# Attention keys in 512-token tiles with both parts one under the other, queries as two tiles with each part twice

## The chip, the cores and the metric

The kernel runs on one core of one Trainium2 chip. The metric is the device time of the program in microseconds (us), as the median of three runs. Its engines are TensorE (PE in the profile; its weight loads are PEld), VectorE (DVE), ScalarE (ACT), GpSimd (POOL) and SyncE (SP), which issues the DMA transfers.

## What is computed

One layer of a streaming encoder, for a prompt of 1024 tokens and for a sample of 64 tokens with cached keys and values. The part that matters here is the first attention. A combined projection gives queries, keys and values for 16 heads of 64 dimensions. Eight heads (A) attend in a band: each 64-frame chunk sees itself and the eight chunks before it. Eight heads (B) are causal over the whole prompt, with a bias from cumulated forget gates. Cut to these lines:

```python
p = rms_norm(x, g_norm1) @ w_in            # q_A k_A v_A | q_B k_B v_B | forget logits
qa, ka = rms_norm(heads(...), g_qa), rms_norm(heads(...), g_ka)     # the same for qb, kb

def attend(q, k, v, bias, mask):
    logits = einsum('bqhd,bkhd->bhqk', q, k) * HEAD_DIM ** -0.5 + bias
    logits = where(mask, logits, -inf)
    return einsum('bhqk,bkhd->bqhd', softmax(logits), v)

# A, prompt: chunk c (64 frames) against frames c*64-512 .. c*64+63, learned relative bias
# B, prompt: query t against frames 0..t, bias cum[t] - cum[s], cum = cumsum(log_sigmoid(forget))
# sample:    64 queries against the cache (512 keys in A, 1024 in B) and the 64 new keys
x = x + concat(oa, ob) @ w_o
x = x + memory_cross_attention(x, mem)     # 4 heads, 256 memory tokens
x = x + conv_ffn(x)
```

The prompt and the sample use the same weights. Keys and values of both go to the outputs too.

## The kernel before

**Parts.** All matmuls run in fp32r, with each operand in two parts: `hi` is the value rounded to fp32r and `lo` is what is left of it. A product of two such values is made of the products hi·hi, hi·lo and lo·hi (in the scores lo·lo as well).

**Head pairs and token tiles.** The prompt's attention goes over eight head pairs `p` (0 to 3 are A, 4 to 7 are B) and eight tiles `t` of 128 tokens. For each, `proj` makes the projection of the tile for the two heads: 24 matmuls into the PSUM bank `pj` (L272, inside `one`). Then `qk_norm` normalizes queries and keys into `qk`, which holds each head's 64 dimensions twice, side by side, so that the transposes in `turn` (L293) give 128 partitions with the dimensions one under the other twice. `gained` (L237 on ScalarE, L238 on VectorE) multiplies them by a gain, rounds them into `hi` and subtracts for `lo`; its last argument limits `lo` to some partitions.

**Groups.** A `Group` holds 256 tokens of a head pair. Keys lie in `kh` (hi in both halves of the partitions) and `kl` (lo in both halves). Queries lie in one tile `q`: hi in partitions 0 to 63, and lo, which is written in place over the second copy, in partitions 64 to 127. One matmul of `q` with `kh` so gives q_hi·k_hi + q_lo·k_hi, and one with `kl` the two other products.

**Scores.** `Attn.score` makes the scores of one tile of 128 queries of a head against its window of `n` keys (up to 640 in A, up to 1024 in B). It walks the key groups of 256 tokens and has two matmuls for each, with `kh` and with `kl` (L453), so at most 256 columns each. They go into `S`, a PSUM tile of two banks that there is only once. A reduction on VectorE (L456) adds the bias, puts the result in `s` and finds the maximum `mx`; ScalarE makes the exponentials (L458). Then come transposes of the probabilities (L493) and the sums with the values.

**Order.** `substeps` cuts the attention of an earlier 256-token group into small functions, and `weave` puts them between the projection matmuls of the next token tile. The last score steps of a pair run beside the next pair's projection. The order on each engine is settled by a scheduler that takes the program in the order of this code and moves instructions by their dependencies. The first pair runs to about 120 us, the others to 571 us.

**Memory and samples.** Next, eight `Sample` units, one for each head pair, and the projection of the memory's keys and values (`mem_piece`, L615) run woven with each other, from about 600 to 722 us. `splitk` takes the cached keys of a head from the input in pieces of 512 tokens; they lie there with the dimensions twice over 128 partitions. ScalarE copies a piece into `kchi` (L709) and VectorE subtracts for `kclo` (L710). `Sample.score` multiplies the two heads' queries (`sq_`, hi over lo, in the trace with a number) with `kchi` of each piece and the new keys' `skn0`, and then with `kclo` and `skn1` (L730, L731). An A sample has one piece for each head, a B sample two. Behind 722 us come the output projection, the memory attention and the ConvFFN.

## Time and profile before

| | |
|---|---|
| three runs | 1797.77, 1800.52, 1801.03 us |
| median | 1800.52 us |
| profiled execution, its own time | 1798.58 us |
| its span, first to last instruction | 1796.5 us |
| mean granted clock of TensorE in it | 0.991 of full speed |

The profile is that of one execution of 1798.58 us. Of this the span is 1796.5 us; the other 2.08 us lie around it. All rows below count from the span's start. A row of a matmul gives its busy time from its start to a modelled end. Since matmuls overlap in the pipeline, the distance from one start to the next is shorter than that time.

### The profile page before, as it was taken

Reading aid. Unit: us, or ns where it says so; the run is one execution under the profiler, and the core shown is the slowest. Engines: PE = TensorE matmul, PEld = TensorE weight load, DVE = VectorE, ACT = ScalarE, POOL = GpSimd, SP = SyncE. Lnnn points to the kernel's source line nnn. Section 1 sums busy time; section 2 is a strip of 40 time slices with the busy share of each in tenths; the row PEclk is TensorE's granted clock in tenths of the full one; section 3 lists DMA queues with packets and bytes.
Section 4 is the critical chain, followed back from the end, with each engine's and each line's share of the span. In section 5 each row is a group of like instructions: output and inputs, shape, how many; then the busy total and the mean of one; then the engine's idle time right before and its main releaser. Section 6 shows DMA issues by size and latency. Waiting matters only on the chain.

```text
span 1796.5 us, 34030 instructions
## 1 busy us (share of the span) xinstructions
PE 1718.8 (96%) x12412; PEld 1663.7 (93%) x12412; DVE 1225.0 (68%) x2710; ACT 930.5 (52%) x2042; POOL 662.8 (37%) x1025
## 2 busy tenths in 40 slices
PE   6899999999997888999999999999999999999999
PEld 5789999999997777999999999999999999999999
DVE  5877667677676797433444379877777777677994
ACT  5646666677676567433554456343333333433332
POOL 5746657878776554453443612100000000000000
PEclk9999999999999999999999999999999999999999
DMA  8312122122113777541111563222222222794232
GB/s 285 96 46 72 36 76 79 50 72 74 48 54 97 222 229 213 163 141 60 54 54 59 150 219 103 73 79 78 85 86 84 73 73 72 268 304 151 77 118 80
DMA packets 134103, 200.12 MB, mean 111 GB/s; under 512 B 20824, under 2 KB 73944, under 8 KB 133936
## 3 DMA queue, kind: packets, MB, share of 16 engines
q1 hardware_dynamic: 133936, 197.96, 34.9%
q8 instruction: 97, 1.59, 0.4%
q14 instruction: 70, 0.57, 0.1%
HBM read 155.61 MB, written 45.44 MB: 112 GB/s over the span
## 4 chain that ended last, share of the span: by engine, by line
PE 46%; DVE 3%; DMA 2%; issue 2%; POOL 1%; ACT 1%; SPq 0%; POOLq 0%; ACTq 0%; DVEq 0%
PE W L1381 25%; PE W L1678 9%; PE pj L869 7%; PE W L869 2%; DMA raw<-in_w_down_dram 1%; PE S L1124 1%; PE tq L1160 1%; PE O L1160 1%; POOL lo L852 1%; DVE lo L1246 0%; PE PT L1147 0%; DVE f L1246 0%; PE O L1124 0%; DMA kvraw<-in_w_down_dram 0%; DMA h<-ad 0%
## 5 line engine op out<-in xcount | busy, mean ns | idle before, releaser
L272 PE MATMUL pj<-whi,xhi 128*128 128x384 f32 (+1 forms) x512 | 194.9, 381 | 8.2 <-ACT xhi L130 7.1
L272 PE MATMUL pj<-wlo,xhi 128*128 128x384 f32 (+1 forms) x512 | 176.9, 346 | 3.2 <-POOL wlo L123 2.9
L272 PE MATMUL pj<-whi,xlo 128*128 128x384 f32 (+1 forms) x512 | 175.1, 342 | 4.2 <-DVE xlo L131 4.2
L1487 POOL COPY s<-gp 128x2 f32<-128x2 f32 x22 | 15.8, 718 | 335.0 <-DVE gp L1486 335.0
L458 ACT ACTIVATE s<-s,mx 128x640 f32<-128x640 f32 (+7 forms) x128 | 94.2, 736 | 80.1 <-DVE mx L456 78.4
L1381 PE MATMUL W<-h,hi 128*128 128x272 f32 x704 | 134.4, 288 | 1.4 <-ACT qlo L1517 1.4
L1678 PE MATMUL W<-f,hi 128*128 128x272 f32 x672 | 128.3, 288 | 3.2 <-DVE f L1246 3.1
L495 DVE TENSOR_TENSOR ptl<-PT,pth 128x512 fp32r<-128x512 f32 (+2 forms) x192 | 99.6, 522 | 37.8 <-ACT pth L494 35.4
L1381 PEld LDWEIGHTS W<-h,hi 128*128 128x128 f32 x704 | 110.8, 188 | 1.7 <-ACT qlo L1517 1.6
L1678 PEld LDWEIGHTS W<-f,hi 128*128 128x128 f32 x672 | 106.0, 189 | 3.8 <-DVE f L1246 3.3
L272 PEld LDWEIGHTS pj<-whi,xhi 128*128 128x128 f32 x512 | 99.5, 195 | 9.3 <-ACT xhi L130 7.1
L224 POOL TENSOR_TENSOR r<-m,mhalf 128x4 f32<-128x4 f32 (+1 forms) x72 | 73.8, 1025 | 91.4 <-DVE m L223 81.3
L272 PEld LDWEIGHTS pj<-wlo,xhi 128*128 128x128 f32 x512 | 99.2, 194 | 5.3 <-POOL wlo L123 4.4
L494 ACT CAST pth<-PT 128x512 fp32r<-128x512 f32 (+2 forms) x192 | 85.1, 449 | 36.9 <-PE PT L493 35.2
L272 PEld LDWEIGHTS pj<-whi,xlo 128*128 128x128 f32 x512 | 97.8, 191 | 5.1 <-DVE xlo L131 5.1
L1381 PE MATMUL W<-h,lo 128*128 128x272 f32 x352 | 101.8, 289 | 0.0
L1245 ACT CAST hi<-raw 128x512 fp32r<-128x512 f32 x68 | 42.2, 621 | 108.8 <-PE W L1381 58.2
L1678 PE MATMUL W<-f,lo 128*128 128x272 f32 x336 | 97.1, 289 | 0.0
L493 PE MATMUL PT<-ident,s 128*128 128x128 f32 x528 | 90.2, 276 | 5.0 <-DVE ptl L495 3.9
L227 POOL TENSOR_SCALAR qk<-qkraw,r 128x128 f32<-128x128 f32 x256 | 92.8, 379 | 6.0
L869 PE MATMUL pj<-a,hi 128*128 128x384 f32 (+1 forms) x352 | 89.5, 337 | 0.3 <-DVE qhi L1005 0.3
L453 PE MATMUL S<-kh,q 128*128 128x256 f32 (+1 forms) x304 | 76.9, 278 | 11.1 <-DVE mx L456 9.6
(604 smaller groups left out, 6053.0 us busy)
## 6 DMA issues: line engine op xcount, KB each, us to landing
raw<-in_w_down_dram SPq DMA_DIRECT2D x45, 256.0 KB, 3.1
wraw<-in_w_dram SPq DMA_DIRECT2D x56, 192.0 KB, 2.4
raw<-in_w_up_dram SPq DMA_DIRECT2D x41, 256.0 KB, 2.8
h<-ad SPq DMA_DIRECT2D x32, 272.0 KB, 4.7
mwraw<-in_w_mkv_dram SPq DMA_DIRECT2D x16, 512.0 KB, 5.1
raw<-in_w_mo_dram SPq DMA_DIRECT2D x32, 256.0 KB, 3.2
kvraw<-in_w_down_dram SPq DMA_DIRECT2D x32, 256.0 KB, 3.2
ad<-t SPq DMA_DIRECT2D x22, 272.0 KB, 2.1
```

The costliest lines, as they stand in the source:

```text
L224: pool.tensor_tensor(r[:rows], m[:rows], mhalf[:rows, 0:4], op=ALU.pow)
L227: pool.tensor_scalar(qk[:rows, h], raw[:rows, h * 64:(h + 1) * 64].rearrange("p (o d) -> p o d", o=1).broadcast_to([rows, 2, 64]), r[:rows ...
L272: pe.matmul(pj[:, :nw], x2[a][:, k, t * P:(t + 1) * P], wt[k][b][:, :nw], start=n == 0, stop=n == 3 * KT - 1)
L453: pe.matmul(sp[:, a:a + (k1 - k0) * P], q, kk[:, h, src], start=m == 0, stop=m == 1)
L458: act.activation(s[:, :n], s[:, :n], ACT.Exp, bias=mx, scale=-1.0, accum_out=sm)
L493: pe.transpose(pt[:, b - ch[0]], self.s[j][:, (b - w0) * P:(b - w0 + 1) * P], ident)
L494: act.copy(hi[:, f:f + n, j], pt[:, f:f + n])
L495: dve.tensor_tensor(lo[:, f:f + n, j], pt[:, f:f + n], f32(hi[:, f:f + n, j]), op=ALU.subtract)
L869: pe.matmul(out()[:, :cn], w[a][:, k % 4], x[b][k][:, c0:c0 + cn], start=k == 0 and n == 0, stop=k == KT - 1 and n == 2)
L1245: act.copy(hi, t)
L1381: pe.matmul(w[:, z, :Q], a(p, j), rights[j][b][:, z * Q:z * Q + Q], start=fresh and begin and j == 0 and x == 0, stop=final and end and j ...
L1678: pe.matmul(ws[m][:, z, :Q], la[p][:, m * P:(m + 1) * P], ra[b][:, z * Q:z * Q + Q], start=first and y == 0 and what in opening, stop=fina ...
```

## The change

In the prompt the keys of 512 tokens lie in one tile `k` (`keys_of`, three buffers in place of five each of `kh` and `kl`): hi in partitions 0 to 63 and lo in 64 to 127. The queries lie in two tiles, `qh` with hi in both halves and `ql` with lo in both halves. A score goes over `qh` and then `ql`, and for each over the key tiles, with up to 512 columns in a matmul. The place `off` in `S` at which a window begins is counted from a tile of 512 tokens, so that no matmul crosses a bank. In the samples, a piece of cached keys is one tile `kc`, hi over lo, in place of `kchi` and `kclo`; the subtraction works in place on partitions 64 to 127. Queries there are two tiles `sq0` and `sq1`, and the new keys one tile `skn`. The four products are the same. Lines behind the first place are 4 higher (L453 becomes L457, L272 becomes L276, L710 and L730 become L713 and L733).

```diff
@@ -202,12 +202,16 @@
 
     class Group:
         def __init__(self):
-            self.kh = wa.tile([P, 2, 256], F32R, name="kh", bufs=5)
-            self.kl = wa.tile([P, 2, 256], F32R, name="kl", bufs=5)
             self.v = wa.tile([P, 2, 2, 2, 64], F32R, name="v", bufs=5)
-            self.q = wa.tile([P, 2, 256], F32R, name="q", bufs=2)
-
-    groups = {}
+            self.q = [wa.tile([P, 2, 256], F32R, name=x, bufs=2) for x in ("qh", "ql")]
+
+    groups, keys = {}, {}
+
+    def keys_of(p, t):
+
+        if (p, t // 4) not in keys:
+            keys[p, t // 4] = wa.tile([P, 2, 512], F32R, name="k", bufs=3)
+        return keys[p, t // 4]
 
     def squares(src, rows):
         sq = wk.tile([P, 256], F32, name="sq", bufs=2)
@@ -293,8 +297,9 @@
                 pe.transpose(tq[:, h], qk[:, h].rearrange("p a d -> p (a d)"), ident)
             c = slice(j * P, j * P + P)
             kind = p // 4
-            gained(g.kh[:, :, c], g.kl[:, :, c], tq[:, 2:4], gd[:, kind, 1:2])
-            gained(g.q[:, :, c], g.q[64:, :, c], tq[:, 0:2], gd[:, kind, 0:1], slice(64, P))
+            k, kc = keys_of(p, t), slice(t % 4 * P, t % 4 * P + P)
+            gained(k[:, :, kc], k[64:, :, kc], tq[:, 2:4], gd[:, kind, 1:2], slice(64, P))
+            gained(g.q[0][:, :, c], g.q[1][:, :, c], tq[:, 0:2], gd[:, kind, 0:1])
             vflat = vf.rearrange("p h d -> p (h d)")
             cols = slice((p % 4) * P, (p % 4) * P + P)
             if p >= 4:
@@ -443,14 +448,13 @@
             else:
                 b = bias[p, h][:, 640 - n:640]
             sp = ps.tile([P, 2, 512], F32, name="S", bufs=1).rearrange("p a b -> p (a b)")
-            off = (w0 % 2) * P
-            q = groups[p, g].q[:, h, j * P:(j + 1) * P]
-            for kg in range(w0 // 2, t // 2 + 1):
-                k0, k1 = max(w0, 2 * kg), min(t, 2 * kg + 1) + 1
-                a = off + (k0 - w0) * P
-                src = slice((k0 - 2 * kg) * P, (k1 - 2 * kg) * P)
-                for m, kk in enumerate((groups[p, kg].kh, groups[p, kg].kl)):
-                    pe.matmul(sp[:, a:a + (k1 - k0) * P], q, kk[:, h, src], start=m == 0, stop=m == 1)
+            off = (w0 % 4) * P
+            for m, qq in enumerate(groups[p, g].q):
+                for kg in range(w0 // 4, t // 4 + 1):
+                    k0, k1 = max(w0, 4 * kg), min(t, 4 * kg + 3) + 1
+                    a = off + (k0 - w0) * P
+                    src = slice((k0 - 4 * kg) * P, (k1 - 4 * kg) * P)
+                    pe.matmul(sp[:, a:a + (k1 - k0) * P], qq[:, h, j * P:(j + 1) * P], keys[p, kg][:, h, src], start=m == 0, stop=m == 1)
             mx = wk.tile([P, 1], F32, name="mx", bufs=4)
             sm = wk.tile([P, 1], F32, name="ssum", bufs=4)
             dve.tensor_tensor_reduce(out=s[:, :n], in0=sp[:, off:off + n], in1=b, scale=-1.0, scalar=BIG,
@@ -688,10 +692,10 @@
             tq = bank("tq").rearrange("p (a b) -> p a b", a=4)
             for x in range(4):
                 pe.transpose(tq[:, x, :S], self.qd[:, x], ident[:S, :S])
-            self.q = mq.tile([P, 2, S], F32R, name="sq_", bufs=2)
-            self.kn = [mq.tile([P, 2, S], F32R, name=f"skn{x}", bufs=2) for x in range(2)]
-            gained(self.q, self.q[64:], tq[:, 0:2, :S], gd[:, p // 4, 0:1], slice(64, P))
-            gained(self.kn[0], self.kn[1], tq[:, 2:4, :S], gd[:, p // 4, 1:2])
+            self.q = [mq.tile([P, 2, S], F32R, name=f"sq{x}", bufs=2) for x in range(2)]
+            self.kn = mq.tile([P, 2, S], F32R, name="skn", bufs=2)
+            gained(*self.q, tq[:, 0:2, :S], gd[:, p // 4, 0:1])
+            gained(self.kn, self.kn[64:], tq[:, 2:4, :S], gd[:, p // 4, 1:2], slice(64, P))
             if p >= 4:
                 b = self.s
                 pool.tensor_scalar(b, b, stok[:, p - 4:p - 3], 1.0, op0=ALU.add, op1=ALU.mult)
@@ -704,11 +708,9 @@
             k = self.kraw.pop(0)
             for c in range(self.nc):
                 raw = k[:, c * 512:(c + 1) * 512]
-                hi = mq.tile([P, 512], F32R, name="kchi", bufs=4)
-                lo = mq.tile([P, 512], F32R, name="kclo", bufs=4)
-                act.copy(hi, raw)
-                dve.tensor_tensor(lo, raw, f32(hi), op=ALU.subtract)
-                self.kc[h, c] = hi, lo
+                kc = self.kc[h, c] = mq.tile([P, 512], F32R, name="kc", bufs=4)
+                act.copy(kc, raw)
+                dve.tensor_tensor(kc[64:], raw[64:], f32(kc[64:]), op=ALU.subtract)
 
         def splitv(self):
             for c in range(self.nc):
@@ -720,15 +722,16 @@
 
         def score(self, h):
             n = self.ctx
-            b, q, r = self.s, self.q.rearrange("p h t -> p (h t)"), slice(h * S, h * S + S)
+            b, r = self.s, slice(h * S, h * S + S)
             if h == 0:
                 self.mx = wk.tile([P, 2], F32, name="smx", bufs=2)
             sp = ps.tile([P, 2, 512], F32, name="S", bufs=1)
             sn = bank("tq").rearrange("p (a b) -> p a b", a=4)
-            for m in range(2):
+            for m, q in enumerate(self.q):
+                q = q.rearrange("p h t -> p (h t)")
                 for c in range(self.nc):
-                    pe.matmul(sp[:, c], q, self.kc[h, c][m], start=m == 0, stop=m == 1)
-                pe.matmul(sn[:, 0, :S], q, self.kn[m][:, h], start=m == 0, stop=m == 1)
+                    pe.matmul(sp[:, c], q, self.kc[h, c], start=m == 0, stop=m == 1)
+                pe.matmul(sn[:, 0, :S], q, self.kn[:, h], start=m == 0, stop=m == 1)
             sf = sp.rearrange("p a b -> p (a b)")
             dve.tensor_tensor_reduce(out=b[r, :n], in0=sf[r, :n], in1=b[r, :n], scale=-1.0, scalar=BIG,
                                      op0=ALU.add, op1=ALU.min, accum_out=self.mx[r, 0:1])
```

The score matmuls of the prompt go from 608 to 384; all other instructions keep their number on each engine. First, on TensorE (PE), a score of 640 keys of an odd tile of the band heads. `pj` is the projection's PSUM bank, `whi` and `xlo` are parts of weights and tokens. Before:

```order
L272 MATMUL pj<-whi,xlo 128x384
L453 MATMUL S<-kh,q 128x128 [waits DVE_49,Activation_49]
L453 MATMUL S<-kl,q 128x128
L453 MATMUL S<-kh,q 128x256
L453 MATMUL S<-kl,q 128x256
L453 MATMUL S<-kh,q 128x256
L453 MATMUL S<-kl,q 128x256
L272 MATMUL pj<-whi,xhi 128x384
```

And now:

```order
L276 MATMUL pj<-whi,xlo 128x384
L457 MATMUL S<-k,qh 128x384 [waits DVE_49,Activation_49]
L457 MATMUL S<-k,qh 128x256
L457 MATMUL S<-k,ql 128x384 [waits DVE_49]
L457 MATMUL S<-k,ql 128x256
L276 MATMUL pj<-whi,xhi 128x384
```

Six matmuls in pairs by key group have become four, the two with `qh` ahead of the two with `ql`. Second, on TensorE too, the cached keys of the first sample's second head and what stands around its score (`mwhi`, `mlo` and the like are parts of the memory's weights and tokens; `sqd` is a sample's queries and keys before their transposes). Before:

```order
L615 MATMUL pj<-mwlo,mhi 128x256
L730 MATMUL S<-kchi,sq__9195 128x512 [waits DVE_49,Activation_49]
L730 MATMUL S<-kchi,sq__9195 128x512 [waits Activation_49]
L615 MATMUL pj<-mwhi,mlo 128x256
L730 MATMUL S<-kclo,sq__9195 128x512 [waits DVE_49]
L615 MATMUL pj<-mwhi,mhi 128x256
L615 MATMUL pj<-mwlo,mhi 128x256
L615 MATMUL pj<-mwhi,mlo 128x256
L730 MATMUL S<-kclo,sq__9195 128x512 [waits DVE_49]
```

And now:

```order
L619 MATMUL pj<-mwhi,mlo 128x256
L733 MATMUL S<-kc,sq_8955 128x512 [waits DVE_49,PE_49]
L694 MATMUL tq<-ident,sqd 128x64 [waits DMAHW6_49]
L694 MATMUL tq<-ident,sqd 128x64 x3
L619 MATMUL pj<-mwhi,mhi 128x256
L733 MATMUL S<-kc,sq_8955 128x512 [waits DVE_49]
L733 MATMUL S<-kc,sq_8956 128x512 x2
L619 MATMUL pj<-mwlo,mhi 128x256
```

The first matmul of each key piece, which waited for ScalarE (Activation) before, waits for VectorE (DVE) now, and the second half follows without a wait. The next unit's transposes (`tq`) have moved in between.

## Rows read from the trace of the kernel before

**Rows 1.** Head of the page: span; busy time, share and instructions by engine.

```profile
span 1796.5 us, 34030 instructions
PE 1718.8 (96%) x12412; PEld 1663.7 (93%) x12412; DVE 1225.0 (68%) x2710; ACT 930.5 (52%) x2042; POOL 662.8 (37%) x1025
```

**Rows 2.** Stretches: us, busy of PE, PEld, DVE, ACT, POOL, granted clock, DMA, GB/s.

```profile
0.00:120.00 120.00, 95.62 (x550) 84.39 (x551) 85.99 (x254) 70.27 (x188) 66.63 (x119) 0.97 0.51 157
120.00:571.00 451.00, 441.87 (x3033) 422.37 (x3032) 317.32 (x900) 309.63 (x796) 325.86 (x594) 1.00 0.21 60
...
600.00:722.00 122.00, 104.29 (x700) 90.68 (x699) 99.28 (x231) 79.83 (x201) 59.57 (x56) 0.94 0.71 223
722.00:1797.00 1075.00, 1060.86 (x8037) 1052.82 (x8035) 703.12 (x1289) 450.20 (x818) 194.61 (x238) 1.00 0.35 112
```

**Rows 3.** The same of L453 alone: PE and PEld busy, clock, DMA, GB/s.

```profile
120.00:571.00 451.00, 75.47 (x510) 73.03 (x510) 1.00 0.21 60
```

**Rows 4.** Waits of PE, 120 to 571 us: total, times, longest.

```profile
PE S L453 <- DVE mx L456: 3.0, 5, 0.8
PE pj L272 <- POOL wlo L123: 2.5, 3, 0.8
```

**Rows 5.** Groups of L453 by shape: count, busy us, mean ns, idle before.

```profile
L453 PE MATMUL S<-kh,q 128*128 128x256 f32 x224 | 61.6, 296 | 10.4 <-DVE mx L456 9.4 <-DVE q L238 0.8
...
L453 PE MATMUL S<-kh,q 128*128 128x128 f32 x80 | 18.2, 227 | 0.8 <-DVE q L238 0.6 <-DVE mx L456 0.2
```

**Rows 6.** Timeline of PE from 147.87 us: start, us, engine, line, operation.

```profile
147.87 0.22 PE L453 MATMUL S<-kh,q 128*128 128x128 f32 x1
147.93 0.27 PE L453 MATMUL S<-kl,q 128*128 128x128 f32 x1
148.04 0.34 PE L453 MATMUL S<-kh,q 128*128 128x256 f32 x1
148.21 0.28 PE L453 MATMUL S<-kl,q 128*128 128x256 f32 x1
148.33 0.28 PE L453 MATMUL S<-kh,q 128*128 128x256 f32 x1
148.45 0.28 PE L453 MATMUL S<-kl,q 128*128 128x256 f32 x1
148.56 0.34 PE L272 MATMUL pj<-whi,xhi 128*128 128x384 f32 x1
148.74 0.34 PE L272 MATMUL pj<-wlo,xhi 128*128 128x384 f32 x1
```

**Rows 7.** Timeline of PE at a sample's score, two matmuls a row.

```profile
658.99 0.63 PE L730 MATMUL S<-kchi,sq__9819 128*128 128x512 f32 x2
659.46 0.77 PE L730 MATMUL S<-kclo,sq__9819 128*128 128x512 f32 x2
```

**Rows 8.** Stretches of PE alone: us, PE busy, granted clock, DMA, GB/s.

```profile
571.00:575.00 4.00, 0.00 (x0) 1.00 0.94 357
575.00:585.00 10.00, 4.47 (x18) 0.50 0.54 174
...
712.00:722.00 10.00, 7.36 (x25) 0.51 0.84 277
```

**Rows 9.** Instructions of L238: count, ns (least, median, most), first and last start, forms.

```profile
L238 DVE SCALAR_TENSOR_TENSOR kl<-tq,gd,kh x64: 468/484/486, 28.2 to 567.9; 128x256 fp32r<-128x256 f32 x64
L238 DVE SCALAR_TENSOR_TENSOR q<-tq,gd,q x64: 490/491/494, 29.3 to 569.2; 64x256 fp32r<-64x256 f32 x64
```

**Rows 10.** Waits of PE, 600 to 722 us: total, times, longest.

```profile
PE S L730 <- DVE kclo L710: 2.7, 4, 0.9
...
PE S L730 <- DVE sq__9568 L238: 1.7, 1, 1.7
...
PE S L730 <- ACT kchi L709: 0.9, 2, 0.5
```

**Rows 11.** L710, 600 to 722 us: count, busy us, mean ns, idle before.

```profile
L710 DVE TENSOR_TENSOR kclo<-kraw,kchi 128x512 fp32r<-128x512 f32 x24 | 21.9, 930 | 2.0 <-ACT kchi L709 1.8
```

## The prediction

> **What bounds the kernel now.** I read the page's busy shares first, then the stretches of the run, then the score matmuls in them, then TensorE's waits where the change touches it. TensorE is busy 96% of the span, 1796.5 us [rows 1]; the whole profiled execution took 1798.58 us. The stretches [rows 2] show three kinds of place. Between 120 and 571 us TensorE is busy 441.87 of 451 us at granted clock 1.00, and 510 of the prompt's 608 score matmuls lie there [rows 3]: what it saves there brings the end of that stretch forward by nearly as much. Its longest waits in it are 3.0 us, in 5 places, for the reduction that frees the score tile S, and 2.5 us for weights [rows 4]. The samples' attention, 600 to 722 us, is another case: TensorE is busy 104.29 of 122, so an operand that comes later can hold it up. Behind 722 us nothing is changed, and TensorE is busy 1060.86 of 1075 us.
>
> **The prompt's scores: fewer and longer matmuls.** The columns streamed stay 135,168. Before there are 448 matmuls of 256 columns and 160 of 128 (half of each with `kh`, as in [rows 5], half with `kl`). After, by the loops, a band head has 6 each of 512, 384, 256 and 128 columns and a forgetting head 12, 4, 4 and 4: 144, 80, 80 and 80 in all, 384 in place of 608. The order shows that the long ones stand in one piece.
>
> The busy mean of one (296 and 227 ns in [rows 5]) is not its price, since matmuls overlap; the price is the step from one start to the next. [Rows 6] shows a whole score of 640 keys between projection matmuls. One of 256 columns is followed after 0.118 us (148.21, 148.33, 148.45, 148.56), one of 384 after 0.175 (148.56, 148.74). The two of 128 start at 147.87 and 147.93, and the score's six take 0.69 us until 148.56; less 4 x 0.118 leaves 0.22, so 0.111 for one of 128, though it has half the columns of the 0.118. So a short matmul hardly costs less than one of 256. For 512 columns the line through 256 and 384 gives 0.232; two of the samples' matmuls of 512, 658.99 to 659.46 [rows 7], give 0.235 each. I take 0.232.
>
> Before: 448 x 0.118 + 160 x 0.111 = 52.9 + 17.8 = 70.7 us. After: 144 x 0.232 + 80 x 0.175 + 80 x 0.118 + 80 x 0.111 = 33.4 + 14.0 + 9.4 + 8.9 = 65.7 us. The saving is 5.0 us (4.6 with 0.235). Most of it is the 80 matmuls of 128 columns that become part of a longer one. At one place: the 0.69 us of [rows 6] become 2 x 0.175 + 2 x 0.118 = 0.59.
>
> What arrives: 510 of 608 lie in the stretch that is 98% busy, and I count those whole. The other 98 carry 98 / 608 x 5.0 = 0.8 us and lie in the first 120 us, busy 95.62 [rows 2], and behind 571 us, where a hole of 4 us without one matmul stands [rows 8]; of theirs I count half. So -4.6 us.
>
> The copies of keys and queries are still made by as many instructions, and one on half the partitions costs no less: 484 ns for 128 partitions, 491 ns for 64 [rows 9]. That the subtraction now serves 64 partitions of the keys and 128 of the queries therefore comes to nothing. A score now begins before the queries' rounded-off part is ready, which only its second half reads; on the other side it needs the key tile's subtraction at its first matmul. In the prompt the newest keys are made ahead of their queries, so neither adds. Sums, transposes and projection keep their instructions.
>
> **The samples' scores** keep their 80 matmuls. Before, the first half of a score read `kchi`, which ScalarE makes, while VectorE still made `kclo` for the second half. Now both halves read one tile `kc`, complete only behind VectorE's subtraction. TensorE waited for `kclo` 4 times, 2.7 us in all, and for `kchi` twice, 0.9 us [rows 10]. What such a score now waits longer is at most what its first half covered: two matmuls of 512 columns for the four samples with 1024 cached keys, one for the other four, so 0.46 or 0.23 us by the 0.232 above. With two heads each the bounds are 0 and 8 x 0.46 + 8 x 0.23 = 5.5 us. The rows are nearer to the low end: 4 of 16 scores waited, so about 4 x 0.35 (between 0.23 and 0.46) = 1.4 us. Against it, TensorE waited 1.7 us once for the queries' low part [rows 10], which the first half no longer needs; I give back 0.7. Net +0.7 us. The subtraction on half the partitions keeps its time (930 ns in the mean, [rows 11]) as that of [rows 9] does. Behind a score that waits stand the memory projection's matmuls and the transposes, on which the same VectorE work waits anyway.
>
> **Sum.** -4.6 + 0.7 = -3.9 us: 1794.7 us against the profiled execution's 1798.58. That lies 1.94 under the median of the runs, 1800.52, and on the median's scale the forecast is 1800.52 - 3.9 = 1796.6 us. Its own range by the terms: with 0.235 for 512 and half of the 0.8 lost -4.2, and 2 us for the samples, -2.2; with 5.0 and no cost for the samples, -5.0. That is 1795.5 to 1798.3.
>
> **Rivals.** First, more comes than the matmuls save. The granted clock is half behind some gaps: after the idle 571 to 575 us it reads 0.50 over 575 to 585, with 4.47 us of busy time, and 0.51 over 712 to 722, with 7.36 [rows 8]; that work would take 2.2 and 3.7 us less at full clock. The change shifts every start behind the first scores, and a gap that closes takes such a stretch with it: -3.9 - 2.2 = -6.1 (1794.4), with the dearer one -7.6 (1792.9). For it: gaps of a few us decide. Against it: the hole at 571 us stands at full DMA load (0.94), so a transfer ends it, which nothing here moves. 0.15.
>
> Second, only columns count. The columns are equal, and if the slot that a short matmul seems to take in [rows 6] is lost elsewhere too, the saving is nearly nothing and the samples' +0.7 stays: 1801.2. For it: from the first 128 to the second it is only 0.06 us, half of 0.118. Against it: the score's 1280 columns took 0.69 us, where by columns they would take 5 x 0.118 = 0.59. 0.2.
>
> On this rival the Trainium skill has a rule (TensorE: Matmul & The Clock Gate, Back-to-back issue gap): an isolated warm matmul takes its columns over 2.4 GHz plus 2.5 ns. By it the 224 matmuls fewer would be worth an estimated 0.6 us, and the time would be 1800.6. The rows don't bear it out for these pairs of weight load and matmul: 0.118 us for 256 columns, where it gives an estimated 0.109, and 0.111 for 128, where it gives 0.056.
>
> Third, slower. Every sample score waits out its subtraction, 5.5 us, and the longer gaps in front of the scores bring one more half-clock stretch with 7.36 us of work as behind 712 us, 3.7 us: -4.6 + 5.5 + 3.7 = +4.6, 1805.1. It ends slower than before from the point where more than 4.6 of these 9.2 us are paid, and measurably so from 8.2. For it: one tile now gates both halves, and the stage has idle time already. Against it: 12 of 16 scores didn't wait for `kclo`, and VectorE is busy 99.28 of 122 us [rows 2], so it has room to run ahead. 0.1.
>
> That the change doesn't do what it says is excluded by the order.
>
> **How the numbers follow.** The forecast has 0.55, the rivals 0.15, 0.2 and 0.1. The likeliest time is 1796.6 us. The range leaves out the third rival and little else: down to the first rival's dearer end with no cost for the samples, 1792.2, rounded to 1792.0; up to the second with 1 us for the samples in place of 0.7, 1801.5. A measurement of this kernel can tell about 0.2%, 3.6 us, from no change. The forecast's -3.9 lies just beyond: of its 0.55 I count 0.33 as faster and 0.22 as within. With the first rival faster has 0.48, with the second within has 0.42, and slower has the third's 0.1.
>
> **What would show it.** The score line should show 144, 80, 80 and 80 matmuls, with 0.23 us from the start of one of 512 to the next. What ends at 571 us should end about 4.5 us earlier. In the samples' stage the scores' waits for VectorE's `kc` should come to 2 to 5 us (2.7 before for `kclo`), the stage stay within 1 us of its 122, and the half-clock stretches be the same ones. I am wrong if a matmul of 512 is followed later than after 0.24 us, if the waits for the score tile grow past 3.0 us by more than 1, or if a new half-clock stretch stands in the samples' stage.

## The result, and the profile after

The change made the kernel slower: 1809.28 us (median of 8 runs, 1806.43 to 1815.84) against 1801.42 us for the kernel before beside it, also of 8 runs (the 1800.52 that the forecast starts from is the median of the first three of them). The ratio is 1.005, with a 95% interval of 1.0037 to 1.0063. The forecast was 1796.6 us and the range ended at 1801.5.

The head of the page after, as [rows 1]; then TensorE in four stretches of the kernel after (us, PE busy, granted clock, DMA share, GB/s). The first three end where the first projection matmul of pair 1's fourth token tile, of pair 4's first and of pair 7's last starts; the fourth is the samples' stage:

```profile
span 1807.3 us, 33632 instructions
...
PE 1720.6 (95%) x12188; PEld 1657.9 (92%) x12188; DVE 1230.3 (68%) x2710; ACT 930.8 (52%) x2042; POOL 664.8 (37%) x1025
```

```profile
0.00:125.90 125.90, 97.57 (x515) 0.92 0.48 150
125.90:303.70 177.80, 170.85 (x1099) 1.00 0.19 56
303.70:560.20 256.50, 250.30 (x1639) 1.00 0.21 62
607.60:724.10 116.50, 102.41 (x687) 0.93 0.70 220
```

The same places in the kernel before:

```profile
0.00:118.30 118.30, 93.92 (x539) 0.97 0.51 159
118.30:292.40 174.10, 171.09 (x1165) 1.00 0.20 57
292.40:551.40 259.00, 254.12 (x1750) 1.00 0.21 62
599.40:714.40 115.00, 98.67 (x686) 0.97 0.70 218
```

The span grew by 10.8 us, and the two tables give most of it: +7.6 up to pair 1's fourth tile, +3.7 in the band pairs, -2.5 in the forgetting pairs, +1.5 in the samples. From the samples' end on, where nothing differs, it is about +1; between 551.4 and 599.4 us it is -0.6. So a gain does come, but only in the forgetting pairs. Most of the loss is in the first 304 us, in stretches where the forecast had only gains. In the samples' stage the mean granted clock is lower too, 0.93 in place of 0.97, where the forecast had the same half-clock stretches.

The score matmuls themselves (as [rows 5]; count, busy us, mean ns, idle before), and a score of 640 keys (start, us), to be held against [rows 6]:

```profile
L457 PE MATMUL S<-k,ql 128*128 128x512 f32 x72 | 29.1, 423 | 0.1
L457 PE MATMUL S<-k,qh 128*128 128x512 f32 x72 | 28.9, 420 | 5.9 <-DVE mx L460 5.8
L457 PE MATMUL S<-k,qh 128*128 128x384 f32 x40 | 14.3, 357 | 0.0
```

```profile
156.08 0.46 PE L457 MATMUL S<-k,qh 128*128 128x384 f32 x2
156.37 0.45 PE L457 MATMUL S<-k,ql 128*128 128x384 f32 x2
156.66 0.34 PE L276 MATMUL pj<-whi,xhi 128*128 128x384 f32 x1
```

A row with x2 holds two matmuls, here one of 384 and one of 256 columns. The score takes 156.66 - 156.08 = 0.58 us, as forecast (0.59), where that of [rows 6] took 0.69. This score costs what it was said to cost. What grew is elsewhere.

### Where the first 7.6 us go

TensorE's waits between 63 and 126 us (total, times, longest), TensorE's stretches behind the first of them, and the row of ScalarE (ACT) that comes before it; then the same row in the kernel before and its TensorE in about the same stretch:

```profile
PE O L512 <- ACT pth L498: 4.3, 1, 4.3
PE tq L392 <- DVE s L384: 2.0, 1, 2.0
```

```profile
66.40:70.90 4.50, 0.25 (x2) 0.88 0.12 34
70.90:77.00 6.10, 6.07 (x24) 0.53 0.14 43
77.00:84.00 7.00, 7.00 (x50) 1.00 0.11 30
```

```profile
66.82 1.06 ACT L146 ACTIVATE s<-s 128x1024 f32<-128x1024 f32 x1 [5.11 <-DMA s<-in_xn_dram]
```

```profile
64.34 1.06 ACT L146 ACTIVATE s<-s 128x1024 f32<-128x1024 f32 x1 [3.04 <-DMA s<-in_xn_dram]
```

```profile
65.00:84.00 19.00, 16.16 (x109) 1.00 0.16 46
```

ScalarE's next instruction in its order is the square of token rows (`stats`, L146), and it stands 5.11 us until their transfer lands at 66.8 us. Behind it in the same queue are the exponentials and the rounding of the probabilities, on which TensorE waits. TensorE is idle for some 4.3 us and then runs 6.1 us at half clock (0.53 in the mean, the lower of its two levels). In the kernel before the same square starts at 64.34 us, TensorE's waits behind it up to 84 us are 1.1 us and less, and the clock stays at 1.00.

Why the rows are issued late is seen on SyncE's queue (start, us, in its order), first in the kernel after, then before:

```profile
55.70 0.34 SPq L309 DMA_DIRECT2D out_ak_dram<-ko  x1
56.09 0.42 SPq L310 DMA_DIRECT2D out_av_dram<-vf  x1
56.57 1.14 SPq L175 DMA_DIRECT2D rows<-in_table_dram  x2
57.87 1.31 SPq L145 DMA_DIRECT2D s<-in_xn_dram  x2
```

```profile
55.09 0.34 SPq L304 DMA_DIRECT2D out_ak_dram<-ko  x1
55.49 1.14 SPq L175 DMA_DIRECT2D rows<-in_table_dram  x2
56.93 2.26 SPq L145 DMA_DIRECT2D s<-in_xn_dram  x2
```

In both kernels the token rows (`in_xn`) are issued behind an output that waits for the tile's keys, and behind two copies of the bias table, 384.5 KB each. In the kernel after that output goes out 0.6 us later, and one more, of the values, stands behind it. So the rows are issued 0.9 us later now, and the square that waits for them starts 2.5 us later. Why 0.9 us at the issue became 2.5 no run shows.

That is not all of the 7.6 us. From 84 us to the end of the first part, first before, then after:

```profile
84.00:118.30 34.30, 30.08 (x191) 0.95 0.23 59
84.00:125.90 41.90, 35.29 (x203) 0.88 0.20 55
```

The clock is lower there too, 0.88 of 41.9 us against 0.95 of 34.3, an estimate of 5.0 us against 1.7 that half clock takes. In this part TensorE waits 2.0 us for `s`, sums of the forget gates (the second of the waits above), and once 1.2 us for `qk`; in the kernel before these are 1.2 and 0.2.

### Where the 3.7 us of the band pairs go

At the last score but one of the second band pair, before and after. First VectorE (DVE) and GpSimd (POOL) before (start, us):

```profile
218.23 0.48 DVE L238 SCALAR_TENSOR_TENSOR kl<-tq,gd,kh 128x256 fp32r<-128x256 f32 x1
218.62 0.41 DVE L222 TENSOR_REDUCE m<-sq 128x4 f32<-128x256 f32 x1
219.06 0.23 DVE L223 TENSOR_SCALAR m<-m,eps 128x4 f32<-128x4 f32 x1
219.20 0.82 DVE L456 CUSTOM_DVE_ANT_0 s<-S,bias 128x640 f32<-128x640 f32 x1
```

```profile
219.25 1.02 POOL L123 TENSOR_TENSOR wlo<-wraw,whi 128x384 fp32r<-128x384 f32 x1 [0.97 <-ACT whi L121]
```

And after:

```profile
228.02 0.49 DVE L242 SCALAR_TENSOR_TENSOR k<-tq,gd,k 64x256 fp32r<-64x256 f32 x1
228.55 0.42 DVE L226 TENSOR_REDUCE m<-sq 128x4 f32<-128x256 f32 x1
229.00 0.96 DVE L227 TENSOR_SCALAR m<-m,eps 128x4 f32<-128x4 f32 x1
229.99 0.82 DVE L460 CUSTOM_DVE_ANT_0 s<-S,bias 128x640 f32<-128x640 f32 x1
```

```profile
228.93 1.00 POOL L123 TENSOR_TENSOR wlo<-wraw,whi 128x384 fp32r<-128x384 f32 x1 [0.97 <-ACT whi L121]
```

Read the starts. Before, the sum of squares (`m`) starts 0.39 us after the keys' subtraction, while that is still running (218.62, end 218.71). After, the subtraction lies on partitions 64 to 127, and the sum starts 0.53 us behind it, once it has ended. The tiny add of eps (the norm's small constant) so moves from 219.06, 0.19 us ahead of GpSimd's subtraction of weights, to 229.00, 0.07 us behind its start. Of these 0.26 us about half is the longer distance on VectorE; the other half is that GpSimd starts sooner behind the keys' subtraction, 0.91 us in place of 1.02. Without these 0.14 us the add would still start ahead of GpSimd, an estimate from the starts. Behind GpSimd's start the add ends only with GpSimd's work: 0.96 us in place of 0.23. The score's reduction stands behind it, and at the end of the chain TensorE waits about 1 us for the low part of the probabilities (`ptl`). That happens once in each band pair, as the waits of TensorE between 126 and 304 us show (in the same window of the kernel before they are 0.8 us in 2 places):

```profile
PE PT L497 <- DVE ptl L499: 2.9, 3, 1.0
```

The Trainium skill has both rules. VectorE: DVE Perf Modes, Two Vector instructions with no wait between them: an instruction whose operands start in another group of 32 partitions than those of the one in front of it starts only when that has finished (the page calls this a model). SBUF — State Buffer, Who interferes with whom: VectorE and GpSimd share a pair of ports, and of two instructions that need it the one that starts first holds it to its end. The rows here agree with both (0.53 against 0.39 us; 0.96 against 0.23).

### The profile page after: what moved, and what is told of

Same layout as the page of the kernel before. It is cut to its first block, busy times and chain, and to the rows that moved or that the text cites. A ratio compares the mean times of both kernels' runs of the same rounds, so it can differ in the third digit from the quotient of the medians.

```text
span 1807.3 us, 33632 instructions
## 1 busy us (share of the span) xinstructions
PE 1720.6 (95%) x12188; PEld 1657.9 (92%) x12188; DVE 1230.3 (68%) x2710; ACT 930.8 (52%) x2042; POOL 664.8 (37%) x1025
## 4 chain that ended last, share of the span: by engine, by line
PE 48%; DMA 2%; DVE 2%; issue 1%; POOL 1%; ACT 1%; SPq 0%; POOLq 0%; ACTq 0%; DVEq 0%
PE W L1384 25%; PE W L1681 11%; PE pj L872 7%; PE W L872 1%; PE S L1127 1%; DMA kvraw<-in_w_down_dram 1%; PE tq L1163 1%; PE O L1163 1%; POOL lo L855 1%; PE PT L1150 0%; DMA raw<-in_w_down_dram 0%; DMA f<-x2d 0%; PE O L1127 0%; DMA h<-ad 0%; PE PT L1108 0%
## 5 line engine op out<-in xcount | busy, mean ns | idle before, releaser
L276 PE MATMUL pj<-whi,xhi 128*128 128x384 f32 (+1 forms) x512 | 193.9, 380 | 7.4 <-ACT xhi L130 6.6
L276 PE MATMUL pj<-wlo,xhi 128*128 128x384 f32 (+1 forms) x512 | 177.3, 347 | 4.7 <-POOL wlo L123 4.3
L276 PE MATMUL pj<-whi,xlo 128*128 128x384 f32 (+1 forms) x512 | 175.9, 344 | 4.9 <-DVE xlo L131 4.9
L276 PEld LDWEIGHTS pj<-whi,xhi 128*128 128x128 f32 x512 | 100.0, 196 | 10.2 <-ACT xhi L130 6.6
L276 PEld LDWEIGHTS pj<-wlo,xhi 128*128 128x128 f32 x512 | 99.4, 194 | 7.9 <-POOL wlo L123 6.2
L276 PEld LDWEIGHTS pj<-whi,xlo 128*128 128x128 f32 x512 | 98.0, 191 | 5.9 <-DVE xlo L131 5.8
L497 PEld LDWEIGHTS PT<-ident,s 128*128 128x128 f32 x528 | 67.1, 142 | 24.3 <-DVE ptl L499 17.0
```

The source lines that it names most:

```text
L276: pe.matmul(pj[:, :nw], x2[a][:, k, t * P:(t + 1) * P], wt[k][b][:, :nw], start=n == 0, stop=n == 3 * KT - 1)
L497: pe.transpose(pt[:, b - ch[0]], self.s[j][:, (b - w0) * P:(b - w0 + 1) * P], ident)
```

## The experiments

The table gives each kernel's stretches, from the starts of the same matmuls in its trace, and its ratio to the kernel before beside it with the 95% interval. "First" ends at pair 1's fourth tile, "band" at pair 4's first, "forget" at pair 7's last; "samples" runs from the memory's first projection matmul to the output projection's first.

| kernel | first | band | forget | samples | span | median | ratio |
|---|---|---|---|---|---|---|---|
| before | 118.3 | 174.1 | 259.0 | 115.1 | 1796.5 | 1801.42 | 1 |
| after | 125.9 | 177.8 | 256.5 | 116.6 | 1807.3 | 1809.28 | 1.0050 (1.0037 to 1.0063) |
| new_form_old_order | 122.4 | 176.9 | 257.3 | 127.8 | 1816.7 | 1813.74 | 1.0081 (1.0066 to 1.0096) |
| old_form_new_order | 123.1 | 174.8 | 257.0 | 113.9 | 1798.3 | 1802.10 | 1.0002 (0.9979 to 1.0026) |
| prompt_part_alone | 123.4 | 178.8 | 256.4 | 118.5 | 1809.9 | 1812.03 | 1.0061 (1.0049 to 1.0073) |
| samples_part_alone | 117.8 | 174.6 | 258.9 | 120.3 | 1799.4 | 1807.24 | 1.0040 (1.0029 to 1.0052) |
| new_queries_first | 121.4 | 174.5 | 256.1 | 115.1 | 1799.3 | 1802.53 | 1.0024 (1.0009 to 1.0039) |
| old_queries_first | 122.6 | 178.1 | 258.2 | 112.6 | 1800.2 | 1803.06 | 1.0020 (1.0007 to 1.0033) |
| new_narrow_matmuls | 120.9 | 178.2 | 258.0 | 119.7 | 1803.8 | 1806.10 | 1.0046 (1.0028 to 1.0064) |
| new_table_rows_later | 122.0 | 178.4 | 256.6 | 117.3 | 1804.4 | 1807.38 | 1.0056 (1.0035 to 1.0077) |
| new_rows_pinned | 118.7 | 178.8 | 256.6 | 117.3 | 1802.1 | 1803.11 | 1.0013 (1.0004 to 1.0022) |
| new_both_cures | 117.1 | 174.5 | 256.2 | 116.6 | 1795.7 | 1798.77 | 0.9991 (0.9980 to 1.0003) |
| old_rows_pinned | 115.4 | 174.5 | 258.9 | 113.9 | 1793.6 | 1796.53 | 0.9979 (0.9969 to 0.9988) |
| new_eps_on_gpsimd | 122.0 | 173.0 | 255.1 | 115.9 | 1797.3 | 1799.17 | 0.9998 (0.9989 to 1.0007) |
| new_eps_rows | 118.1 | 172.3 | 255.2 | 116.2 | 1792.8 | 1794.54 | 0.9974 (0.9963 to 0.9985) |
| old_eps_rows | 117.4 | 173.1 | 261.4 | 114.3 | 1795.2 | 1796.73 | 0.9988 (0.9975 to 1.0000) |
| new_three | 118.4 | 171.4 | 254.2 | 118.5 | 1790.9 | 1794.07 | 0.9976 (0.9964 to 0.9987) |

The stretches come from one profiled execution each. For new_form_old_order it took 1818.74 us, 5 over the median, for samples_part_alone 1801.30, 6 under it. The forgetting heads, where three kernels have the old form in the old order, take 259.0, 258.9 and 258.9 us; a difference of 3 or 4 us counts, one of 0.5 does not. In the samples' stage it takes more: prompt_part_alone, whose samples have the old form, has 118.5 us there, 3.4 over the kernel before.

### Order or form

The first theory was that the other order costs the time. A list that holds each instruction's place, pinned by dependencies within an engine, gives either kernel the other's order:

```diff
     in_order(tc)
+    as_listed(tc)
...
+        for a, b in zip(at, at[1:]):
+            tc.add_manual_dep(mine[b], mine[a].name, mybir.DependencyInfo(
+                mybir.DependencyClass.NoSync, mybir.DependencyReason.DATA), reason="order")
```

> The changed kernel, with every engine's instructions put in the order in which they stand in the kernel before (a score's fewer matmuls stand where the first of its matmuls stood). Theory A, order: the fewer matmuls do save their 4 to 5 us, and the loss of 8 us comes from the other order that the scheduler settled on (345 places on TensorE, 286 on VectorE, 176 on ScalarE, 75 on GpSimd, 32 on SyncE). Then this is 1796 to 1798 us, 4 us under before, the hole of 4.3 us at 66 us and the half clock behind it are gone. Theory B, form: the wide matmuls, the subtraction on 64 partitions in place or the one tile that gates both halves cost the time themselves. Then this stays at 1806 to 1810 us.

> The kernel before, with every engine's instructions in the order of the changed kernel (a score's narrow matmuls stand together where its wide ones stand). Theory A, order: it gets the new order's loss without the gain: 1810 to 1814 us. Theory B, form: 1800 to 1803 us, as before.

Both came out against the theory: the new form in the old order is slower still (1813.74), and the old form in the new order is as fast as before (1802.10). Order alone loses 4.8 us in the first part and gives 2 back in the forgetting pairs. The form alone, in the old order, loses 4.1 us in the first part, so neither has that loss to itself; it gives 1.7 back in the forgetting pairs, and with it stay 2.8 us of the band pairs. What makes new_form_old_order so slow is one more thing, in its samples' stage, 127.8 us long. There TensorE waits for the subtraction 13 times, in 10 of the 16 scores, where the kernel after waits 4 times. Of each the waits (total, times, longest), new_form_old_order first:

```profile
PE S L733 <- DVE kc L713: 14.6, 13, 2.0
```

```profile
PE S L733 <- DVE kc L713: 1.3, 4, 0.4
```

So one tile for both halves does gate the samples' scores, as the third rival had it, and dearer than its bound of 5.5 us, but only in an order made for the old form. The scheduler's new order avoids it.

With the same order on every engine, the two traces can be laid instruction upon instruction. That is how the place above was found: in new_form_old_order TensorE falls behind the kernel before by 1.04 us at one transpose in each band pair, behind such a slow add.

### One part alone

> Only the prompt's keys and queries changed, the samples as before. The trace of the changed kernel is 9.0 us late where the prompt's projection ends and 9.6 where the samples' stage ends, so both theories expect nearly the whole loss here: 1807 to 1809 us. If it comes out near 1801, the samples' part moved something in the prompt's order, and the loss is its.

> Only the samples' keys and queries changed, the prompt as before. From the 0.6 us between the end of the prompt's projection and the end of the samples' stage: 1801 to 1803 us, not to be told from before. If it is slower by more than 4 us, the gate of both halves on the subtraction (bound 5.5 us in the prediction) is paid in full.

These two have the first hunks of the diff without those of the class `Sample`, and those alone. The prompt's part carries the loss, as expected, and more of it: 1812.03 us where at most 1809 was said, +5.1 in the first part and +4.7 in the band pairs. The samples' part alone was expected to be free and costs 0.4%, 1807.24 us. The trace is of little help here, since its execution took only 1801.30 us: the stage takes 120.3 us in it, with 5.3 us of waits for `kc`, 4.0 of them in one place. Together with the prompt's part, the samples' stage is at 116.6. What the samples' form costs thus hangs on the order, perhaps also on when the stage begins; the two parts don't add up.

### The subtraction on 64 partitions

```diff
-            gained(k[:, :, kc], k[64:, :, kc], tq[:, 2:4], gd[:, kind, 1:2], slice(64, P))
             gained(g.q[0][:, :, c], g.q[1][:, :, c], tq[:, 0:2], gd[:, kind, 0:1])
+            gained(k[:, :, kc], k[64:, :, kc], tq[:, 2:4], gd[:, kind, 1:2], slice(64, P))
```

The same two lines are exchanged in the kernel before for old_queries_first. In new_narrow_matmuls the loop over the keys goes by groups of 256 tokens again, with the tiles of the change:

```diff
-                for kg in range(w0 // 4, t // 4 + 1):
-                    k0, k1 = max(w0, 4 * kg), min(t, 4 * kg + 3) + 1
+            for kg in range(w0 // 2, t // 2 + 1):
+                k0, k1 = max(w0, 2 * kg), min(t, 2 * kg + 1) + 1
...
```

> The changed kernel with its queries multiplied, rounded and split ahead of its keys (two lines of turn() exchanged). From the fourth tile of pair 1 to the first of pair 4 the kernel before takes 174.1 us, the changed one 177.9, the changed one in the old order 176.8; there PE waits about 1 us in each pair for the low part of the probabilities, behind an add of eps that took 0.96 us on VectorE beside GpSimd's subtraction of weights, where it took 0.23. Theory C: the subtraction on 64 partitions holds VectorE's next instruction back 0.13 us longer than that on 128, and since the change it stands ahead of the adds, so that they fall into GpSimd's work. Then with the queries first that stretch takes 174 to 175.5 us, and the whole 1804 to 1806 us. Rival: it is the long matmuls that make the scores late; then the stretch stays at 177 to 178 us.

> The kernel before with its queries ahead of its keys, so that there too the subtraction on 64 partitions stands first. Theory C: the stretch from the fourth tile of pair 1 to the first of pair 4 grows from 174.1 to 176.5 to 178 us, and the whole to 1803 to 1805 us. Rival: with its narrow matmuls it stays at 174 to 175 us.

> The changed kernel's tiles, copies and subtractions, but score matmuls of at most 256 columns as before (608 in all, the two halves of a group of keys one behind the other). Theory C: the loss of the band heads stays (stretch 177 to 179 us) and the gain of the forgetting heads goes: from pair 4's first tile to pair 7's last it takes 258 to 260 us, as before (259.0), where the changed kernel takes 256.5. The whole is 1809 to 1813 us. Rival, the long matmuls are the cost: 1800 to 1802 us.

In the stretches all three fit. With the queries first the loss of the band pairs goes, 177.8 to 174.5 us. The kernel before, which has none of the change, gets the whole of it from the same exchange, 174.1 to 178.1. And with narrow matmuls it stays at 178.2, while the gain of the forgetting pairs shrinks from 2.5 to 1.0 us. The whole came out lower than expected twice: 1802.53 us with the queries first (1804 to 1806 was said), and 1806.10 with narrow matmuls (1809 to 1813), which is no slower than the kernel after (ratio 1.0046 against 1.0050). So the whole time does not show that the long matmuls are worth anything. In old_queries_first VectorE's rows at the second band pair read as those of the kernel after, with its own old tiles (GpSimd's subtraction starts at 225.59):

```profile
224.69 0.49 DVE L238 SCALAR_TENSOR_TENSOR q<-tq,gd,q 64x256 fp32r<-64x256 f32 x1
225.21 0.42 DVE L222 TENSOR_REDUCE m<-sq 128x4 f32<-128x256 f32 x1
225.67 0.97 DVE L223 TENSOR_SCALAR m<-m,eps 128x4 f32<-128x4 f32 x1
```

The other way to cure it leaves the keys first and moves the add:

```diff
-        dve.tensor_scalar(m[:rows], m[:rows], eps_ap, None, op0=ALU.add)
+        pool.tensor_scalar(m[:rows], m[:rows], eps_ap, 1.0, op0=ALU.add, op1=ALU.mult)
```

> The changed kernel, keys first, with the add of eps in the norm on GpSimd, so that VectorE has no small add that can fall beside GpSimd's subtraction of the weights. Theory C: the stretch from the fourth tile of pair 1 to the first of pair 4 comes down from 177.9 to 174 to 175.5 us, though the subtraction on 64 partitions still stands first. If it stays at 177 to 178, the add is not what makes the scores late.

The band pairs take 173.0 us, below the kernel before, and the whole is level with it (0.9998). Of these 4.8 us some 1 to 1.4 are a gain that the old form has from the same cure (old_eps_rows, 173.1 us against 174.1 and 174.5); the rest is the loss. So the chain is held from both ends: without the 64 partitions in front, or without the add, the loss is gone.

### The token rows

```diff
-            if t == 3 and p < 3:
+            if t == (6 if p == 0 else 3) and p < 3:
                 load_rows(p + 1)
```

> The changed kernel with the second pair's copies of the bias table (three quarters of a megabyte of transfers, in memory) issued three tiles later, behind the token rows that ScalarE waits for at 61.7 to 66.8 us in the changed kernel and until 64.3 in the kernel before. Theory D: in the first pair the loss of 7 to 8 us until the fourth tile of pair 1 hangs on this wait: ScalarE stands, TensorE waits 4.3 us behind it and runs at half clock for some 6 us after. With the rows landed earlier the fourth tile of pair 1 starts at 120 to 122 us in place of 126.0, and the whole takes 1802 to 1805 us. Rival: the wait only takes another place, and the tile starts at 125 to 127 us.

This moved the lines and not the instructions: the scheduler issued the table's copies ahead of the token rows all the same (56.42 and 57.72 us), and the rows landed at 65.8. That its first part is 3.9 us shorter than in the kernel after so proves nothing on the cause; at most it shows how much that part varies with where the holes fall. The next run pinned the copies in addition:

```diff
-            nc.sync.dma_start(rows[head], i["table"][head:head + 1].broadcast_to([P, 769]))
+            d = nc.sync.dma_start(rows[head], i["table"][head:head + 1].broadcast_to([P, 769]))
+            if p == 1:
+                tc.keep_in_program_order(d)
```

> The changed kernel with the second pair's copies of the bias table held back on SyncE's queue, behind the first pair's seventh tile (in the run before, their place in the text was moved, and the scheduler put them ahead of the token rows all the same: issued at 56.4 us, the rows at 57.7). Theory D: the token rows then land before 62 us in place of 66.8, ScalarE doesn't stand, TensorE's wait of 4.3 us for the probabilities and the half clock behind it go, and the fourth tile of pair 1 starts at 119 to 122 us in place of 125.9 (before: 118.3). Rival, the wait passes on to another operand: it starts at 124 to 126.

Now the copies stand behind the rows, on SyncE's queue, and TensorE's stretch from 65 to 84 us (PE busy, granted clock) reads first as in the kernel after, then as in new_rows_pinned:

```profile
57.22 1.34 SPq L145 DMA_DIRECT2D s<-in_xn_dram  x2
...
61.37 1.15 SPq L175 DMA_DIRECT2D rows<-in_table_dram  x2
```

```profile
65.00:84.00 19.00, 14.73 (x82) 0.82 0.17 47
```

```profile
65.00:84.00 19.00, 18.19 (x119) 1.00 0.25 76
```

The 4.3 us wait and the half clock are gone, 37 matmuls more fit into these 19 us, and the first part takes 118.7 us in place of 125.9: to the kernel after the pin is worth 7.2 us. The other kernels with late rows (65 to 66 us) lie at 121 to 124 us, with holes of 1.5 to 3.5 us and behind them half-clock stretches as long as here (new_form_old_order, old_queries_first) or shorter; how dear the delay comes depends on where the holes fall.

> The changed kernel with the queries ahead of the keys and with the copies of the bias table held back. If the two losses are separate: first part until pair 1's fourth tile 117 to 120 us (before 118.3), from there to pair 4 174 to 175 (174.1), pairs 4 to 7 256 (259.0), and the whole 2 to 4 us under before, 1795 to 1798 us. If the two cures take away the same thing, as both lower the first part, it starts at 121 us and the whole is as before.

> The kernel before with the copies of the bias table held back in the same way, as a measure of what that is worth without the change: ScalarE waits until 64.3 us for the token rows there, and TensorE has 2.2 us of waits behind it without half clock. Theory D: 0 to 2 us less, 1798 to 1800 us. If it gains 4 us or more, the cure is worth as much without the change, and the change's part in the loss is smaller than I say.

The two losses are separate. With both cures the first part and the band pairs are as before or better. The whole of new_both_cures is only level with the kernel before, though (0.9991), where 2 to 4 us less was expected. And the kernel before gains 3.2 us from the pinned copies too, more than the 0 to 2 expected, since it waited at the same place, only less. Its first part goes from 118.3 to 115.4 us. So of the 7.6 us the late rows explain 4.3, and 118.7 - 115.4 = 3.3 are left with the copies pinned in both. They lie behind 84 us; old_rows_pinned, then new_rows_pinned:

```profile
84.00:115.40 31.40, 25.92 (x165) 0.95 0.24 60
84.00:118.70 34.70, 28.69 (x163) 0.85 0.21 55
```

The clock alone, 0.85 of 34.7 us against 0.95 of 31.4, is an estimate of 5.2 us against 1.6, as it was without the pin. What makes these half-clock stretches, no run has tested.

So the comparison that counts has the cures on both sides:

> The changed kernel with both cures that left its form alone: the add of eps on GpSimd and the copies of the bias table held back. If the parts add up: 117 to 119 us until pair 1's fourth tile, 173 to pair 4, 255 through the forgetting heads, and the whole 1791 to 1795 us, 5 to 8 us under before.

> The kernel before with the same two cures. Theory: the change is worth its matmuls, so this is 2 to 5 us over new_eps_rows, by 2 to 4 us in the forgetting heads (257 to 259 us against 255) and 0 to 1 us in the band heads: 1794 to 1798 us. Rival: the cures alone make all the gain, and the two kernels end within 1.5 us of each other.

> The changed kernel with both cures and the queries ahead of the keys. With the add off VectorE the order of the two should hardly matter: band heads 172.5 to 174 us, the whole within 2 us of new_eps_rows. If it is slower by more, the keys' place ahead of the queries is worth something that the add hid.

With the add moved and the copies pinned, the changed kernel is 1796.73 - 1794.54 = 2.2 us ahead, near the low end of what was expected. That does not show what the change is worth. The two ratios' intervals overlap, and with the other pair of cures it is the old form that leads by 2.2 us: old_rows_pinned, which has its subtraction on 128 partitions first already, takes 1796.53 us and new_both_cures 1798.77. The best of the old form (0.9979) and the best of the new (0.9974) can't be told apart. The ratio of 0.9974 to the kernel before (0.9963 to 0.9985) does make new_eps_rows faster than both kernels of the case, and new_three (0.9976) is level with it. The queries' place does not matter once the add is off VectorE. The page head of new_eps_rows, to be held against that of the kernel after:

```profile
span 1792.8 us, 33654 instructions
...
PE 1709.7 (95%) x12188; PEld 1653.9 (92%) x12188; DVE 1210.1 (67%) x2638; ACT 929.7 (52%) x2042; POOL 681.0 (38%) x1097
```

VectorE has 72 instructions and 20 us less. old_eps_rows lost 2.4 us in its forgetting pairs against before (261.4 us; 257 to 259 was expected). TensorE waits there for GpSimd, which now has the adds as well, 4.9 us in 7 places, where the kernel before has 0.8 us in one and new_eps_rows 1.6 in one:

```profile
PE pj L274 <- POOL wlo L123: 4.9, 7, 1.5
```

So this cure costs the old form something that it doesn't cost the new, and a part of the 2.2 us may be that.

## Why the prediction was wrong

The count of matmuls, 608 to 384, was right, and the long ones were priced right: 0.23 us from one of 512 to the next. (Behind the 40 of the 144 that have one of 128 next the step is 0.28, over the 0.24 that was to show the forecast wrong; the one of 128 then takes only 0.06, so that the two together cost what was said.) The **saving was too large by a quarter**. A short matmul's price was read from one score in which it stands first; where the 128 columns stand last the two cost 0.17 us together and not 0.22. Measured over each kind of score, from its first start to the next instruction's (medians, before less after): the scores of 640 keys of the band heads, eight each, 13, 62, 65 and 13 ns; the forgetting heads' scores of 640 to 1024 keys, eight each, 14, 83, 71 and 31; the short ones of 128 to 512 keys, sixteen each, 2, 2, 60 and 7. That is 1.2 + 1.6 + 1.1 = 3.9 us where 5.0 was said. The 62 is the middle of two groups: four such scores save 0.11 us, as the one shown above, and four only 0.01.

"**I count those whole**" is not shown even for the forgetting pairs. Their gain is 2.5 us, where the terms above give 8 x 0.199 + 8 x 0.071 = 2.2; but the old form in the new order has 2.0 of it with none of the long matmuls, and at equal order the form is worth 1.7 (old) or 0.5 us (new). In the band pairs it did not hold: other waits took the gain and more.

The step that failed is the sentence that the copies' change of partitions "**comes to nothing**". It weighed the two durations in [rows 9], 484 and 491 ns, and these did not change. What changed is when the next instruction may start, 0.39 or 0.53 us later, and which of the two stands ahead of the small adds. This is not seen in a duration but in the distance between starts. The two exchanges of keys and queries measure the term: +3.3 us in the kernel after, +4.0 in the kernel before, in the place of 0.

The second failing step is not in the sum at all. **What lies before 120 us** was counted as half of a small gain. That TensorE is idle for 24 of 120 us there was read as room; it means as well that this stretch hangs on transfers and on ScalarE's queue, where a delay of 0.9 us at SyncE became 2.5 at the landing, 1.4 more of idle time on TensorE between 65 and 84 us (19.00 - 14.73 = 4.3 against 19.00 - 16.16 = 2.8), and an estimated 3 in half clock (6.1 us less 0.53 of it). That agrees with the 4.3 of the 7.6 us that go when both kernels have the copies pinned; the 3.3 that are left go with longer half-clock stretches behind 84 us, and their cause stays open. The first rival had the half-clock stretches right as a mechanism and named only the gain from one that closes; here new ones opened.

The samples came out near the forecast in the kernel after: +1.5 us, with 1.3 us of waits for `kc` in 4 places, where +0.7 and 2 to 5 us of waits were said. That is partly luck: the stage's clock fell from 0.97 to 0.93 in the mean, which the forecast had the same, and prompt_part_alone, with the old samples, lost 3.4 us there. The third rival, slower than before, had the right sign and the wrong place: its gate on `kc` was paid in full only in new_form_old_order. The second rival, that only columns count, fell by the 3.9 us that the scores themselves are shorter, though not by any whole time.

Not settled: the 3.3 us of the first part; about 1 us behind the samples' stage, where the change has left the instructions alone and the profiled executions lie between 1079.9 and 1085.5 us; and why the samples' part alone costs 0.4%.

## What to carry to other kernels

A tile that is cut differently changes not only how long a copy takes but when its neighbour may begin: look at the distance from start to start on the engine that does the copy, and at what stands next in its queue and on the engine beside it. In a stretch where the bounding engine is idle a fifth of the time, find the transfer that ends the longest wait and ask how late it may come; here 4.3 us of loss went with an issue 0.9 us later. And when a change comes out slower than its terms, give both kernels the same order first, because two traces with one order can be compared instruction by instruction. Give both the same cures as well before pricing a change, and more than one pair of them: here one pair put the change 2.2 us ahead and another 2.2 us behind.

## What was new on the hardware

An add on 128 x 4 elements took 0.96 us in place of 0.23 when it started 0.07 us behind a 1.00 us subtraction on GpSimd. A VectorE instruction on all partitions, behind one on partitions 64 to 127, started 0.53 us after that one's start, and behind one on all partitions 0.39, though both took 0.48 to 0.49. And a wait of 4.3 us of TensorE was followed by 6.1 us at a granted clock of 0.53, an estimated 3 us lost, two thirds of the wait again.
